# Retention with the wide product for q and k, split value products, and conversions queued behind normed rows at the hand-overs between stages

## The chip, the cores and the metric

The kernel runs on one core of a Trainium2 chip, in one launch. Its time is device microseconds (us) of that core. Before the change it takes 1206.07 us, the median of 3 runs (1205.51 to 1206.59). A core has five engines that run side by side, each through its own instructions in order: TensorE (PE, matrix products and transposes), VectorE (DVE), ScalarE (ACT), GpSimd (POOL) and SyncE (SP, which issues the transfers from memory). PEld is the part of TensorE that loads weights.

## The reference

Two transformer blocks over 256 tokens of width 1024, in fp32. The first mixes tokens with four kinds of attention and has an MLP; the second has a retention layer with a feed-forward part, and then a sparse-attention layer with another. Around each mixer and each feed-forward part stand a root-mean-square norm and a residual. What the change touches in the arithmetic is the retention layer:

```
proj = x @ w_in
q, k, v, g = split(proj)             # 4 heads; q, k 256 wide, v, g 512 wide
q = rotate_pairs(q, cos, sin)
k = rotate_pairs(k, cos, sin) * 256 ** -0.5
# chunks of 128 tokens:
scores = einsum('bhid,bhjd->bhij', qc, kc) * intra_decay
o = einsum('bhij,bhje->bhie', scores, vc) + (product with the state of the chunk before)
o = o * rsqrt(mean(o * o) + eps)     # per head
return (o * silu(g)) @ w_out
```

## The kernel before

**Split products.** fp32 matrix products are made of a high and a low part of each operand, both in the type fp32r. `each_half` (L225) fetches a piece of a weight (SP, tile `raw`, four buffers), ACT writes its high part (`whi`, L234) and DVE the low part (`wlo`, L237); there are six buffers of such pairs in the pool `wsp`, and some calls bring a private pool besides. `mm3` (L246) makes one product from three: L249, L250, L251. `ws_chunk` uses it with the weight as the stationary operand and 256 tokens as columns (N=256). `ws_wide` (L259) does the same with two matmuls: the high weight against the high and low tokens side by side (N=512, L268) and the low weight against the high tokens (N=256, L270); then ACT copies one half of the sum (L271) and DVE adds the other (L272).

**Norms and columns.** `a(t)` of a normed input takes the sum of squares of 128 tokens' rows (ACT L399, L401, DVE L404, L407, POOL L409), and DVE L193 and ACT L194 write the normed rows `xn`. `b(t)` transposes them on PE (L429), and for each of 8 columns ACT (L209) and DVE (L210) write high and low part with the norm's gain. In front of w_kv the rows serve two norms, and `b` writes two sets of columns.

**Hand-over between stages.** `project_back` (L350) multiplies back to width 1024. Its last weight halves are held: first they are run for tokens 0, then `residual(0)` (L442, or L451 and L454 with a norm) and `a(0)`; then for tokens 1, with `b(0)` ahead of the last half; then `residual(1)` and `a(1)`. The next stage is `an_groups` (L290): eight weight halves, j = 0 to 7, each with two pieces of `wlo`. It runs the first of them for tokens 0 and calls `b(1)` ahead of the last for which there is room, then tokens 1. This hand-over occurs five times: w_out to w_up, w_down to w_rv, w_ro to w_fi, w_fo to w_kv, w_no to w_fi.

**Order.** A scheduler puts each engine's instructions into one order when the program is built; on the chip each engine runs them in that order. `issue_after` fixes that an instruction stands behind another.

**Retention.** For each of four heads q and then k come from `ws_chunk` (w_rqk) and are rotated (DVE L1111, L1113, POOL L1114). The scores of a head (PE L1120, L1122, DVE L1123, an fp32 product) stand behind the next head's q. Then, for each head, the gates (w_rg, ACT L1138) and the value products (PE L1148, L1150, fp32, N=512), each of which is two instructions on PE.

Of the kernel before, what the change touches and what calls it, by code (L numbers as in the profile page):

```python
# [12 lines left out]
F32 = mybir.dt.float32  # L13
F32R = mybir.dt.float32r
BF = mybir.dt.bfloat16
AF = mybir.ActivationFunctionType
OP = mybir.AluOpType
AX = mybir.AxisListType

T = 256  # L20
# [192 lines left out]
class Kernel:  # L213
# [76 lines left out]
    def an_groups(self, groups, n, inp, order=(0, 1), extra=0):  # L290

        with ExitStack() as es:
            pool = self.pool(es, "ax_" + groups[0][0], extra) if extra else None
            hs = []
            for i, (name, g) in enumerate(groups):
                for j in range(4):
                    if j % 2 == 0:
                        own = {s: pool for s in range(2) if len(hs) + s + extra >= 4 * len(groups)}  # L300
                        chunk = self.each_half(name, 2 * g + j // 2, 4 * n, own, 2)
                    hs.append((i, 2 * j, next(chunk)))
            out = [[self.bank()[:, :n] for _ in range(2)] for _ in groups]

            def mul(j, t):
                i, k0, (hi, lo) = hs[j]
                for k in (k0, k0 + 1):
                    c = slice((k % 2) * n, (k % 2 + 1) * n)
                    self.as_mm(out[i][t], inp.x[0], k, (hi[:, c], lo[:, c]), k == 0, k == KT - 1, t)

            room = min(WSP + extra, len(hs))
            for j in range(room):
                if j == room - 1:
                    inp.b(1)
                mul(j, order[0])
            for j in range(len(hs)):
                if j >= room:
                    mul(j, order[0])
                mul(j, order[1])
        return out  # L320
# [29 lines left out]
    def project_back(self, name, nk, get, last, residual, nxt):  # L350


        accs = [[self.bank() for _ in range(2)] for _ in range(2)]
        n = nk // 2
        held = []
        with ExitStack() as es:
            wx = self.pool(es, "wx_" + name, 2 * last)
            for c in range(n):
                x, k0 = get(c)
                for s, half in enumerate(self.halves(name, c, pools={i: wx for i in range(2) if c >= n - last})):  # L360
                    a = (x, k0 + s, half, c == 0 and s == 0, c == n - 1 and s == 1)
                    if c < n - last:
                        for t in range(2):
                            self.as_t(accs[t], *a, t)
                    else:
                        held.append(a)
            for t in range(2):
                for banks in ((0,), (1,)) if t == 0 or not nxt else ((0, 1),):
                    for a in held[:-1]:
                        self.as_t(accs[t], *a, t, banks)  # L370
                    if t and nxt:
                        nxt.b(0)
                    self.as_t(accs[t], *held[-1], t, banks)
                residual(t, accs[t])
                if nxt:
                    nxt.a(t)


    def gain(self, name):
# [76 lines left out]
    def warm_up(self):  # L456
# [4 lines left out]
        for _ in range(WARM):  # L461
            self.nc.tensor.matmul(ps, w[:, :128], w, start=True, stop=True)

    def behind(self, engine):

        last = next(i for i in reversed(self.nc.cur_bb.bb.instructions) if i.engine == engine.engine)
        return self.tc.issue_after(last)


    def run(self):  # L470
        nc = self.nc
        with ExitStack() as es:
            self.cp = self.pool(es, "cp")
            self.wraw = self.pool(es, "wraw", RAW)
            self.wsp = self.pool(es, "wsp", WSP)
            self.rp = self.pool(es, "rp", 1)
            self.gp = self.pool(es, "gp", 3)
            self.xp = self.pool(es, "xp", 1)
            self.st = self.pool(es, "st", 3)
            self.scr = self.pool(es, "scr", 2)  # L480
            self.jp = self.pool(es, "jp", 1)
            self.ps = self.pool(es, "ps", 8, bass.MemoryType.PSUM)
            nc.scalar.preload_act_table_set("natural_log_exp_and_others")
            self.x = self.rp.tile([128, 2, D], F32, name="res")
            nc.sync.dma_start(self.x[:, 0, :], self.I["x"][:, 0, :])
            self.gc = self.cp.tile([128, len(PRE) * KT], F32, name="gc")
            nc.sync.dma_start(self.gc, self.I["gain_cols"])
            inp = Inputs(self, ("mix_norm_g",))
            cm = self.cp.tile([128, 512], F32, name="cm")
            nc.sync.dma_start(cm[:, :128], self.I["c_mat"][:, :128])  # L490
            self.ident, self.uge, self.ule, self.ones = [cm[:, i * 128:(i + 1) * 128] for i in range(4)]
            self.mhalf = self.cp.tile([128, 8], F32, name="mhalf")
            nc.gpsimd.memset(self.mhalf, -0.5)
            self.warm_up()
            inp.a(0)
            nc.sync.dma_start(self.x[:, 1, :], self.I["x"][:, 1, :])
            inp.b(0)
            inp.a(1)
            mx = self.mix(inp, cm)
            with ExitStack() as e1:  # L500
                inp = Inputs(self, ("mlp_norm_g",), (self.pool(e1, "xq0"),))
                self.project_back("w_out", KT, lambda c: (mx, 2 * c), 3, self.add_residual, inp)
                inp = self.mlp(inp)
            inp = self.retention(inp)
            with ExitStack() as e1:
                xq = self.pool(e1, "xq")
                inp = self.ffn(inp, 0, Inputs(self, ("kv", "pre1"), (None, xq)))
                inp = self.nsa(inp, xq)
            self.ffn(inp, 1, None)
# [564 lines left out]
    def retention(self, inp):  # L1074
        nc, I = self.nc, self.I
        mm = nc.tensor.matmul
        with ExitStack() as es:
# [27 lines left out]
                    pass  # L1105
            at = cp.tile([128, 4, 384], F32, name="at")

            def rotated(s, ps):
                a = tp.tile([128, 2, T], F32, tag=f"rot{s}", name="rot")
                b = tp.tile([128, 2, T], F32, tag="rotb", name="rotb")  # L1110
                nc.vector.tensor_tensor(a, ps, cs, op=OP.mult)  # L1111
                for j in range(2):
                    nc.vector.tensor_tensor(b[:, j, :], ps[:, 1 - j, :], sn[:, j, :], op=OP.mult)  # L1113
                nc.gpsimd.tensor_tensor(a, a, b, op=OP.add)  # L1114
                return a

# [9 lines left out]
            for h in range(4):  # L1126
                rot = []
                for s in range(2):
                    rot.append(rotated(s, self.ws_chunk("w_rqk", 2 * h + s, xin)))
                    if s == 0 and qk:  # L1130
                        scores(h - 1, *qk)
                qk = rot
            ys = []

            def gates(g):
                sg = tp.tile([128, 2, 512], F32, tag="sg", name="sg", bufs=1)
                for _ in self.an_steps("w_rg", g, 512, xin,
                                       lambda t, ps: nc.scalar.activation(sg[:, t, :], ps, AF.Silu)):  # L1138
                    pass
                return sg  # L1140

            def outputs(g, sg):
                vs = slice(g * 512, (g + 1) * 512)
                ss = self.st.tile([128, 2], F32, tag="ss2", name="ss2")
                po = []
                for t in range(2):
                    p = self.bank()
                    mm(p, at[:, g, t * 128:t * 128 + 128], v[:, 0, vs], start=True, stop=t == 0)  # L1148
                    if t:
                        mm(p, at[:, g, T:384], v[:, 1, vs], start=False, stop=True)  # L1150
                    junk = self.jp.tile([128, 2, 512], BF, tag="junk", name="junk")
                    nc.scalar.activation(junk[:, 0, :], p, AF.Square, accum_out=ss[:, t:t + 1])
                    po.append(p)
                r = self.rstd(ss, 512)
                yn = []
                for t in range(2):
                    u = up.tile([128, 512], F32, tag="yn", name="yn")
                    nc.vector.scalar_tensor_tensor(u, po[t], r[:, t:t + 1], sg[:, t, :], op0=OP.mult, op1=OP.mult)
                    yn.append(u)
                return yn  # L1160
# [7 lines left out]
            yn = None  # L1168
            for g in range(4):
                sg = gates(g)  # L1170
                if g == 0:
                    scores(3, *qk)
                else:
                    transposed(yn)
                yn = outputs(g, sg)

            e1.close()

# [408 lines left out]
```

## Time and profile before

| | |
|---|---|
| median of 3 runs | 1206.07 us (1205.51 to 1206.59) |
| profiled execution | 1207.36 us, its span 1205.5 us |
| granted TensorE clock, mean | 0.996 |
| PE busy | 1185.9 us, 98% |
| DVE busy | 799.0 us, 66% |
| ACT busy | 652.8 us, 54% |
| POOL busy | 80.1 us, 7% |

The profile is one execution; the span is from its first instruction to its last. Busy time is the time in which an engine runs at least one instruction. Matmuls overlap: an N=512 product is listed with some 390 ns, while the next starts sooner. So PE's pace is read from starts. "Idle before" names the time an engine waited ahead of an instruction and what released it. The granted clock is 1.00 at 2.4 GHz and 0.50 at 1.2 GHz.

### The profile page before, as it was taken

The page shows a single profiled execution, that of the slowest core. Times are in us where ns is not written, and L with a number is a line of the kernel's source. Part 1 is how long each engine was busy: PE and PEld are TensorE (multiplying, and loading weights), DVE is VectorE, ACT ScalarE, POOL GpSimd, SP SyncE. Part 2 cuts the span into 40 slices and gives each one's busy share as a digit, 9 for nine tenths or more (in the row PEclk, how much of TensorE's full clock was granted, in tenths as well). Part 3 has the DMA queues.
Part 4 walks back from the last instruction along what each step waited for, and adds up shares of the span by engine and source line. Part 5 has one row for each costly group of instructions (what it writes and reads, how often), then busy time and mean ns, then how long its engine had stood idle before and what let it go on. Part 6 is the DMA issues. An engine that isn't in the chain of part 4 may idle for free.

```text
span 1205.5 us, 18575 instructions
## 1 busy us (share of the span) xinstructions
PE 1185.9 (98%) x7104; PEld 1026.5 (85%) x7104; DVE 799.0 (66%) x1381; ACT 652.8 (54%) x1116; POOL 80.1 (7%) x87
## 2 busy tenths in 40 slices
PE   8999999999999999999999999999999999999997
PEld 6999999996888888899778888888889877888886
DVE  7757876557756668657556665657778967656663
ACT  6545764535544455543555554456567876645561
POOL 1000002100000000012000000000100530000000
PEclk8999999999999999999999999999999999999999
DMA  7654464446556666554546355556655226555560
GB/s 250 198 176 145 141 206 145 158 140 213 176 177 188 188 202 200 192 190 157 172 143 220 113 194 189 191 186 208 208 188 187 71 69 211 177 190 190 185 203 35
DMA packets 60777, 210.14 MB, mean 174 GB/s; under 512 B 7120, under 2 KB 9808, under 8 KB 60560
## 3 DMA queue, kind: packets, MB, share of 16 engines
q1 hardware_dynamic: 60688, 208.95, 53.5%
q8 instruction: 56, 0.92, 0.3%
q14 instruction: 33, 0.27, 0.1%
HBM read 207.84 MB, written 1.08 MB: 173 GB/s over the span
## 4 chain that ended last, share of the span: by engine, by line
PE 79%; DVE 8%; DMA 5%; ACT 5%; issue 2%; POOL 1%; SPq 0%; DVEq 0%; POOLq 0%; ACTq 0%
PE b L249 17%; PE b L251 17%; PE b L250 17%; PE b L268 13%; PE b L270 7%; DVE wlo L237 3%; ACT whi L234 2%; PE b L429 1%; DMA raw<-w_up 1%; PE b L1520 1%; DMA wng<-w_ng 1%; ACT s L1487 1%; PE b L1503 1%; PE b L1148 1%; DMA raw<-w_kv 1%
## 5 line engine op out<-in xcount | busy, mean ns | idle before, releaser
L237 DVE TENSOR_TENSOR wlo<-raw,whi 128x1024 fp32r<-128x1024 f32 (+3 forms) x432 | 474.3, 1111 | 267.2 <-ACT whi L234 264.2
L234 ACT ACTIVATE whi<-raw 128x1024 fp32r<-128x1024 f32 (+1 forms) x384 | 401.5, 1050 | 399.1 <-issue 118.7
L249 PE MATMUL b<-whi,x 128*128 128x512 f32 (+1 forms) x752 | 296.0, 395 | 4.0 <-ACT whi L234 2.5
L250 PE MATMUL b<-wlo,x 128*128 128x512 f32 (+1 forms) x752 | 292.8, 390 | 0.2
L251 PE MATMUL b<-whi,x 128*128 128x512 f32 (+1 forms) x752 | 291.9, 389 | 0.1
L268 PE MATMUL b<-x,whi 128*128 128x512 f32 x768 | 270.8, 396 | 0.0
L270 PE MATMUL b<-x,wlo 128*128 128x256 f32 x768 | 215.2, 280 | 0.0
L249 PE MATMUL b<-x,whi 128*128 128x256 f32 x736 | 210.9, 287 | 1.0 <-ACT x L242 1.0
L251 PE MATMUL b<-x,wlo 128*128 128x256 f32 x736 | 207.9, 283 | 0.4 <-DVE wlo L237 0.4
L250 PE MATMUL b<-x,whi 128*128 128x256 f32 x736 | 207.7, 282 | 0.0
L249 PEld LDWEIGHTS b<-whi,x 128*128 128x128 f32 x752 | 141.8, 189 | 38.0 <-ACT x L209 4.7
L268 PEld LDWEIGHTS b<-x,whi 128*128 128x128 f32 x768 | 144.2, 188 | 34.5
L251 PEld LDWEIGHTS b<-whi,x 128*128 128x128 f32 x752 | 141.7, 188 | 30.9 <-DVE x L243 1.2
L250 PEld LDWEIGHTS b<-wlo,x 128*128 128x128 f32 x752 | 142.0, 189 | 30.2 <-DVE wlo L237 2.4
L270 PEld LDWEIGHTS b<-x,wlo 128*128 128x128 f32 x768 | 144.7, 188 | 0.9
L249 PEld LDWEIGHTS b<-x,whi 128*128 128x128 f32 x736 | 140.4, 191 | 3.9 <-issue 2.0
L251 PEld LDWEIGHTS b<-x,wlo 128*128 128x128 f32 x736 | 140.5, 191 | 0.6 <-DVE wlo L237 0.6
L250 PEld LDWEIGHTS b<-x,whi 128*128 128x128 f32 x736 | 140.5, 191 | 0.2
L409 POOL TENSOR_TENSOR rstd<-ms,mhalf 128x1 f32<-128x1 f32 x22 | 14.1, 640 | 690.2 <-DVE ms L407 690.2
L210 DVE SCALAR_TENSOR_TENSOR x<-b,gc,x 128x128 fp32r<-128x128 f32 x112 | 36.8, 348 | 19.2 <-ACT x L209 17.2
L209 ACT ACTIVATE x<-b,gc 128x128 fp32r<-128x128 f32 x112 | 38.2, 368 | 19.5 <-PE b L429 14.7
L1487 ACT ACTIVATE s<-s,nm 128x128 f32<-128x128 f32 (+1 forms) x64 | 28.3, 446 | 2.6 <-DVE rz L1491 1.4
(269 smaller groups left out, 930.3 us busy)
## 6 DMA issues: line engine op xcount, KB each, us to landing
raw<-w_fi SPq DMA_DIRECT2D x88, 512.0 KB, 4.5
raw<-w_fo SPq DMA_DIRECT2D x44, 512.0 KB, 4.5
raw<-w_gate SPq DMA_DIRECT2D x32, 512.0 KB, 3.7
raw<-w_up SPq DMA_DIRECT2D x32, 512.0 KB, 4.7
raw<-w_down SPq DMA_DIRECT2D x32, 512.0 KB, 4.6
raw<-w_qk SPq DMA_DIRECT2D x24, 512.0 KB, 4.0
raw<-w_rv SPq DMA_DIRECT2D x16, 512.0 KB, 5.0
raw<-w_rqk SPq DMA_DIRECT2D x16, 512.0 KB, 4.5
```

What stands on the lines that cost most here:

```text
L209: k.nc.scalar.activation(hi, ps[:, j, :], AF.Copy, scale=g)
L210: k.nc.vector.scalar_tensor_tensor(lo, ps[:, j, :], g, hi.bitcast(F32), op0=OP.mult, op1=OP.subtract)
L234: nc.scalar.activation(hi[:, :n], r, AF.Copy)
L237: nc.vector.tensor_tensor(lo[:, c], r[:, c], hi[:, c].bitcast(F32), op=OP.subtract)
L249: mm(out, lhs[0], rhs[0], start=start, stop=False)
L250: mm(out, lhs[0], rhs[1], start=False, stop=False)
L251: mm(out, lhs[1], rhs[0], start=False, stop=stop)
L268: mm(ps.rearrange("p a t -> p (a t)"), half[0][:, s], x[2][:, k].rearrange("p a t -> p (a t)"), start=k == 0, stop=False)
L270: mm(ps[:, 0], half[1][:, s], x[0][:, k, :], start=False, stop=k == KT - 1)
L409: nc.gpsimd.tensor_tensor(r, ms, self.mhalf[:, :1], op=OP.pow)
L429: self.nc.tensor.transpose(ps[:, j, :], src[:, j * 128:(j + 1) * 128], self.ident)
L1487: nc.scalar.activation(s[:, a, i, :], s[:, a, i, :], AF.Exp, bias=nm[:, a, i:i + 1], scale=-1.0, accum_out=z[:, a, i:i + 1])
```

## The change

Three things. First, the retention's q and k come from `ws_wide`; since its result lies in SBUF and not in a PSUM bank, the rotation reads it there. Second, the value products are made with `mm3`: in `gates`, behind the first weight half, both value tiles and the scores are split in high and low parts, in the buffers of the rotation; the last head's scores stand there too, behind that first half. Third, `project_back` notes the last ACT and DVE instruction of `a(0)` ("a") and of `b(0)` ("b"). In the next `an_groups` the conversions j = 2 to 4 are put behind "a", those from 5 on behind "b"; `residual(1)` and `a(1)` are put behind "b" as well. Ahead of the first `an_groups` no step is noted, and it stays as it is.

```diff
@@ an_groups
                 for j in range(4):
+                    queued = self.conversions_behind(len(hs))
...
-                    hs.append((i, 2 * j, next(chunk)))
+                    with queued:
+                        hs.append((i, 2 * j, next(chunk)))
@@ project_back
                     if t and nxt:
                         nxt.b(0)
+                        self.steps["b"] = self.lasts()
                     self.as_t(accs[t], *held[-1], t, banks)
-                residual(t, accs[t])
-                if nxt:
-                    nxt.a(t)
+                with self.queued(self.steps["b"] if t and nxt else ()):
+                    residual(t, accs[t])
+                    if nxt:
+                        nxt.a(t)
+                if nxt and not t:
+                    self.steps["a"] = self.lasts()
@@ new helpers
+    def lasts(self):
+        order = list(reversed(self.nc.cur_bb.bb.instructions))
+        return [next(i for i in order if i.engine == e.engine) for e in (self.nc.scalar, self.nc.vector)]
+    def queued(self, instructions):
+        es = ExitStack()
+        for i in instructions:
+            es.enter_context(self.tc.issue_after(i))
+        return es
+    def conversions_behind(self, j):
+        return self.queued(self.steps.get("a" if j < 5 else "b", ()) if j > 1 else ())
@@ retention
-            def rotated(s, ps):
-                a = tp.tile([128, 2, T], F32, tag=f"rot{s}", name="rot")
+            def rotated(s, i):
+                a = self.ws_wide("w_rqk", i, xin, tp.tile([128, 2, T], F32, tag=f"rot{s}", name="rot"))
                 b = tp.tile([128, 2, T], F32, tag="rotb", name="rotb")
-                nc.vector.tensor_tensor(a, ps, cs, op=OP.mult)
                 for j in range(2):
-                    nc.vector.tensor_tensor(b[:, j, :], ps[:, 1 - j, :], sn[:, j, :], op=OP.mult)
+                    nc.vector.tensor_tensor(b[:, j, :], a[:, 1 - j, :], sn[:, j, :], op=OP.mult)
+                nc.vector.tensor_tensor(a, a, cs, op=OP.mult)
...
-                    rot.append(rotated(s, self.ws_chunk("w_rqk", 2 * h + s, xin)))
+                    rot.append(rotated(s, 2 * h + s))
...
             def gates(g):
                 sg = tp.tile([128, 2, 512], F32, tag="sg", name="sg", bufs=1)
+                parts = None
                 for _ in self.an_steps("w_rg", g, 512, xin,
                                        lambda t, ps: nc.scalar.activation(sg[:, t, :], ps, AF.Silu)):
-                    pass
-                return sg
+                    if parts is None:
+                        if g == 0:
+                            scores(3, *qk)
+                        src = [v[:, t, g * 512:(g + 1) * 512] for t in range(2)] + [at[:, g, :]]
+                        parts = []
+                        for tag, x in zip(("rot0", "rot1", "rotb"), src):
+                            hl = [...]
+                            self.split(*hl, x)
+                            parts.append(hl)
+                return sg, parts
...
-                    mm(p, at[:, g, t * 128:t * 128 + 128], v[:, 0, vs], start=True, stop=t == 0)
+                    self.mm3(p, [x[:, t * 128:t * 128 + 128] for x in w], v0, True, t == 0)
                     if t:
-                        mm(p, at[:, g, T:384], v[:, 1, vs], start=False, stop=True)
+                        self.mm3(p, [x[:, T:384] for x in w], v1, False, True)
```

In the kernel after the change the lines L399 to L454 stand 6 further on (L442 is L448, L401 is L407, L404 is L410), and L1054 is L1078; L193, L194, L209, L210, L234 and L237 stay.

DVE at the hand-over from w_down to w_rv, before, from the first normed row (L193) on; x_4937 are the columns of the new input, res the residual:

```order
L193 TENSOR_SCALAR xn<-res,rstd 128x512
L210 SCALAR_TENSOR_TENSOR x_4937<-b,gc,x_4937 128x128 x3
L442 TENSOR_TENSOR res<-res,b 128x512
L210 SCALAR_TENSOR_TENSOR x_4937<-b,gc,x_4937 128x128 x2
L442 TENSOR_TENSOR res<-res,b 128x512
L210 SCALAR_TENSOR_TENSOR x_4937<-b,gc,x_4937 128x128 x2
L404 ISA junk,ss<-res 128x512
L404 ISA ss 128x1
L210 SCALAR_TENSOR_TENSOR x_4937<-b,gc,x_4937 128x128
L407 TENSOR_SCALAR ms<-ss 128x1
L237 TENSOR_TENSOR wlo<-raw,whi 128x512
```

The same place on DVE after the change:

```order
L193 TENSOR_SCALAR xn<-res,rstd 128x512
L237 TENSOR_TENSOR wlo<-raw,whi 128x512 x4
L210 SCALAR_TENSOR_TENSOR x_4937<-b,gc,x_4937 128x128 x2
L237 TENSOR_TENSOR wlo<-raw,whi 128x512
L210 SCALAR_TENSOR_TENSOR x_4937<-b,gc,x_4937 128x128 x2
L237 TENSOR_TENSOR wlo<-raw,whi 128x512
L210 SCALAR_TENSOR_TENSOR x_4937<-b,gc,x_4937 128x128 x4
L448 TENSOR_TENSOR res<-res,b 128x512 x2
L237 TENSOR_TENSOR wlo<-raw,whi 128x512
L410 ISA junk,ss<-res 128x512
```

Six pieces of conversion have moved in among the eight columns, and the residual's two adds, which stood between columns, stand behind the last of them.

ACT at the hand-over from w_fo to w_kv, before, from the normed row (L194) of tokens 0 to that of tokens 1; x_8359 and x_8360 are the two sets of columns:

```order
L194 ACTIVATE xn<-res,rstd 128x512
L209 ACTIVATE x_8359<-b,gc 128x128 x3
L399 ACTIVATE junk,ss<-b 128x512
L209 ACTIVATE x_8359<-b,gc 128x128 x2
L401 ACTIVATE junk,ss<-b 128x512
L209 ACTIVATE x_8359<-b,gc 128x128 x2
L209 ACTIVATE x_8360<-b,gc 128x128
L209 ACTIVATE x_8359<-b,gc 128x128
L399 ACTIVATE junk,ss<-res 128x512
L209 ACTIVATE x_8360<-b,gc 128x128 x6
L194 ACTIVATE xn<-res,rstd 128x512
```

The same place on ACT after the change, with the two sets named x_8343 and x_8344:

```order
L194 ACTIVATE xn<-res,rstd 128x512
L234 ACTIVATE whi<-raw 128x1024 x3
L209 ACTIVATE x_8343<-b,gc 128x128 x8
L209 ACTIVATE x_8344<-b,gc 128x128 x8
L405 ACTIVATE junk,ss<-b 128x512
L407 ACTIVATE junk,ss<-b 128x512
L234 ACTIVATE whi<-raw 128x1024
L405 ACTIVATE junk,ss<-res 128x512
L242 ACTIVATE wg<-wng 128x8x48
L194 ACTIVATE xn<-res,rstd 128x512
```

Three conversions now stand ahead of the columns, and the sums of squares of tokens 1 behind all sixteen of them.

## Rows read from the trace of the kernel before

**Rows 1.** The page's chain that ended last: share of the span by engine

```profile
PE 79%; DVE 8%; DMA 5%; ACT 5%; issue 2%; POOL 1%; SPq 0%; DVEq 0%; POOLq 0%; ACTq 0%
```

**Rows 2.** Windows: stretch, then its length, busy us (instructions) by engine, clock, DMA

```profile
515.00:590.00 75.00, 75.00 (x517) 69.49 (x516) 45.33 (x53) 30.29 (x33) 14.67 (x8) 1.00 0.55 176
586.00:645.00 59.00, 59.00 (x258) 45.17 (x257) 32.43 (x38) 31.38 (x50) 2.80 (x4) 1.00 0.45 143
```

**Rows 3.** Timeline of PE, q and k: start, duration, engine, line, operation

```profile
528.93 0.28 PE L251 MATMUL b<-x,wlo 128*128 128x256 f32 x1
...
540.46 0.28 PE L251 MATMUL b<-x,wlo 128*128 128x256 f32 x1
```

**Rows 4.** Timeline of PE, wide products of w_fi

```profile
702.31 0.28 PE L270 MATMUL b<-x,wlo 128*128 128x256 f32 x1
...
707.62 0.28 PE L270 MATMUL b<-x,wlo 128*128 128x256 f32 x1
```

**Rows 5.** Groups by line, 700 to 840: count, busy, mean ns, idle before

```profile
L271 ACT ACTIVATE sg<-b 128x256 f32<-128x256 f32 x18 | 6.6, 367 | 0.5 <-PE b L270 0.5
...
L272 DVE TENSOR_TENSOR sg<-b,sg 128x256 f32<-128x256 f32 x17 | 7.1, 418 | 0.0
```

**Rows 6.** Timeline of PE, value products of head 0

```profile
586.94 1.88 PE L1148 MATMUL b<-v,at 128*128 128x512 f32 x4
588.66 1.02 PE L1150 MATMUL b<-v,at 128*128 128x512 f32 x2
```

**Rows 7.** Timeline of DVE, ACT and PE, w_down to w_rv

```profile
468.05 2.55 DVE L237 TENSOR_TENSOR wlo<-raw,whi 128x512 fp32r<-128x512 f32 x4 [1.58 <-ACT whi L234]
470.51 1.28 DVE L442 TENSOR_TENSOR res<-res,b 128x512 f32<-128x512 f32 x2
...
476.65 0.48 DVE L193 TENSOR_SCALAR xn<-res,rstd 128x512 f32<-128x512 f32 x1 [0.66 <-POOL rstd L409]
...
480.52 0.68 DVE L442 TENSOR_TENSOR res<-res,b 128x512 f32<-128x512 f32 x1
...
487.45 0.49 DVE L193 TENSOR_SCALAR xn<-res,rstd 128x512 f32<-128x512 f32 x1 [0.73 <-POOL rstd L409]
...
477.95 1.94 ACT L209 ACTIVATE x<-b,gc 128x128 fp32r<-128x128 f32 x5 [0.57 <-PE b L429]
...
477.29 1.06 PE L429 MATMUL b<-cm,xn 128*128 128x128 f32 x8 [0.59 <-DVE xn L193]
...
488.00 1.09 PE L429 MATMUL b<-cm,xn 128*128 128x128 f32 x8
```

**Rows 8.** Timeline of ACT and PE, w_fo to w_kv

```profile
864.42 1.15 ACT L209 ACTIVATE x<-b,gc 128x128 fp32r<-128x128 f32 x3 [1.75 <-PE b L429]
...
866.70 0.61 ACT L401 ACTIVATE junk<-b 128x512 bf16<-128x512 f32 x1
...
873.47 0.72 ACT L194 ACTIVATE xn<-res,rstd 128x512 f32<-128x512 f32 x1 [0.38 <-POOL rstd L409]
...
874.37 1.09 PE L429 MATMUL b<-cm,xn 128*128 128x128 f32 x8
...
878.44 0.50 PE L249 MATMUL b<-whi,x 128*128 128x512 f32 x1 [0.83 <-ACT x L209]
```

**Rows 9.** Timeline of ACT and PE, w_out to w_up

```profile
290.86 1.06 ACT L234 ACTIVATE whi<-raw 128x1024 fp32r<-128x1024 f32 x1 [3.77 <-DMA raw<-w_up]
...
291.32 0.39 PE L251 MATMUL b<-whi,x 128*128 128x512 f32 x1
...
298.79 0.40 PE L251 MATMUL b<-whi,x 128*128 128x512 f32 x1
```

**Rows 10.** Windows of PE at the start: length, busy (instructions), clock, DMA

```profile
5.50:9.00 3.50, 0.03 (x1) 0.82 0.95 348
9.00:14.50 5.50, 5.50 (x18) 0.50 0.84 291
```

More of the change, by code (lines that the diff above doesn't have):

```diff
@@ L482, in run @@
             self.ps = self.pool(es, "ps", 8, bass.MemoryType.PSUM)
+            self.steps = {}
             nc.scalar.preload_act_table_set("natural_log_exp_and_others")
@@ L1136, in gates, with outputs @@
                 sg = tp.tile([128, 2, 512], F32, tag="sg", name="sg", bufs=1)
+                parts = None
                 for _ in self.an_steps("w_rg", g, 512, xin,
                                        lambda t, ps: nc.scalar.activation(sg[:, t, :], ps, AF.Silu)):
-                    pass
-                return sg
-            def outputs(g, sg):
-                vs = slice(g * 512, (g + 1) * 512)
+                    if parts is None:
[4 more added lines that the diff above has]
+                        for tag, x in zip(("rot0", "rot1", "rotb"), src):
+                            hl = [tp.tile([128, 2, T], F32, tag=tag, name=tag).rearrange("p a t -> p (a t)").bitcast(F32R)
+                                  [:, :x.shape[1]] for _ in range(2)]
+                            self.split(*hl, x)
+                            parts.append(hl)
+                return sg, parts
+            def outputs(g, sg, parts):
+                v0, v1, w = parts
                 ss = self.st.tile([128, 2], F32, tag="ss2", name="ss2")
@@ L1170, in retention @@
                 sg = gates(g)
-                if g == 0:
-                    scores(3, *qk)
-                else:
+                if g:
                     transposed(yn)
-                yn = outputs(g, sg)
+                yn = outputs(g, *sg)
             e1.close()
```

## The prediction, made before the changed kernel ran

> **What bounds the kernel now.** I read the page first. Its chain of waits runs through TensorE (PE) for 79% of the span [rows 1], and no other engine has more than a tenth of it. So a change here is worth what it takes off PE's instructions, plus what it does to the few moments at which PE stands still. The busy times by stretch come second: in the retention's q and k stage and in its output stage PE has no gap at all, while VectorE (DVE) is busy 45.33 of 75 us and 32.43 of 59 us, and ScalarE (ACT) less [rows 2]. Work added to those two engines is hidden there, and only PE's instructions count. Third come the timelines of PE, DVE and ACT around the places where `project_back` hands over to `an_groups`. There PE does wait: 0.59 us for DVE's first half of the normed rows before w_rv [rows 7], 0.83 us for a column before w_kv [rows 8]. The reader should see that these are small, and that the engines run their instructions in the written order: what is put ahead of a normed row or a column delays it.
>
> **q and k.** The old form runs three N=256 products for each of 16 halves x 8 steps = 128 steps. From 528.93 to 540.46 stand 96 of them, 32 trios, so a trio is 11.53 / 32 = 0.360 us [rows 3]. The wide pair runs elsewhere in this kernel: 15 pairs from 702.31 to 707.62, 0.354 each [rows 4]. 128 x 0.006 = -0.8 us. The wide form adds an ACT copy (0.37) and a DVE add (0.42) for each of 16 halves [rows 5], 5.9 and 6.7 us, on engines with 45 and 30 us free in that stretch. The rotation now waits for the add before it starts, about 1 us later per head, but the scores that need it stand a whole chunk of q, 16 pairs or 5.7 us, behind it. For the last head they now stand behind the first half of the gates. Bounds: -1.0 (the pair a little quicker) to +1.6 (the scores wait 0.4 for each of four heads, one DVE add). I take -0.8, since the idle time is large.
>
> **Value products.** Each head has three fp32 products with N=512, two PE instructions each: four take 586.94 to 588.66, 0.43 each, so six take 2.58 and four heads 10.3 us [rows 6]. After it there are nine fp32r products per head, 36 in all. An N=512 one is the wide pair less an N=256 one, 0.354 - 0.120 = 0.234 [rows 3, 4], so 8.4 us: -1.9 us. The splits are three conversions per head on each of ACT and DVE, at some 0.65 us for 512 columns (four such pieces take 2.55 [rows 7]): 2 us per head beside 13 us of gates. Bounds: -2.5 to 0 (PE then waits as long for a split as it saves).
>
> **The queueing.** Five hand-overs are touched. What is removed is work ahead of the first normed rows; what is added stands ahead of the columns, and behind these now stand residual(1) and a(1), whose rows b(1) transposes. PE runs `b(1)` before the last half that fits, so PE waits for whatever comes late there.
>
> *w_out to w_up.* ACT's half of the normed rows stood behind a conversion that had idled 3.77 us for its DMA [rows 9]. From 291.32 to 298.79 PE starts 21 N=512 products and 8 transposes: 21 x 0.23 + 1.1 = 5.9 of 7.47 us, so 1.6 us are waits [rows 7, 9]. The conversion now stands behind; I take -1.6 (bounds -1.6 and 0).
>
> *w_down to w_rv.* Four pieces of conversion held DVE from 468.05 until the residual could start at 470.51 [rows 7]. They go behind the row, so the row comes up to 1.15 us sooner, and PE's 0.59 us wait goes. But then ACT runs three conversions, 3 x 1.05, before the first column. Its half of the row now ends at about 476.2, the conversions at 479.4, eight columns at 0.39 each (five took 1.94 [rows 7]) at 482.5; DVE's eight, with its own pieces between them, end near 483.4. Before, the residual's second add was already running at 480.52, between the columns; now both wait for the last column, and the second starts at about 484.0, 3.5 us later. From that add to the row it was 6.93 us [rows 7]. The three columns that stood in it (0.9) are gone, two more conversion pieces (1.2) are in it: row at 491.2 or later, the transposes half a us behind, 491.9 where they had begun at 488.00. PE has nothing else in its order: +3.9 us, which swallows the early gain. Bounds: -0.6 (only the wait goes) to +5.
>
> *w_kv.* Here b writes two sets of columns, 16 on each engine. ACT was free from 862.67, 1.75 before the column at 864.42 [rows 8]. Three conversions end at 865.8, 16 columns at 0.39 at 872.1, and only then come the sums of squares that before ran between columns; L401 (now L407) starts near 872.9 instead of 866.70. From there to the row it was 6.77 us with ten DVE columns of about 0.3 in between [rows 8]; without these, and with three conversion pieces of 0.6, 5.6 us: row at about 878.5 to 879.0, transposes at 879.4 against 874.37. That is +5.0, of which 0.9 us only replaces the wait at 878.44 [rows 8]: +4.1. Bounds: -0.9 to +5.5.
>
> *The two w_fi hand-overs.* They have the same order with two halves of private space, so PE reaches b(1) later. Nearest rows: 0 where the slack covers all, +3.9 as at w_rv. I take +1.0 each, +2.0.
>
> **Sum.** -0.8 - 1.9 - 1.6 + 3.9 + 4.1 + 2.0 = +5.7 us. The profiled execution took 1207.36 us, 1.29 above the median of 1206.07, its span 1205.5; the difference is carried over to the median: 1211.8.
>
> **Rivals.**
>
> *Only the waits go.* If the conversions fit into gaps of DVE and ACT behind the rows, and b(1) still comes in time, the hand-overs give -1.6, -0.6, -0.9 and nothing at w_fi, with -2.7 from retention: -5.8, 1200.3. For it: ACT and DVE are both far from full, and the rows do come sooner. Against it: before, these conversions already ran while the engines had nothing else (DVE's four pieces end with the add behind them); the change takes that time away and puts the work where columns and rows compete.
>
> *Break-even.* The columns come late by half of what I work out: +4.2 at the hand-overs, -4.3 from w_out and the retention, 1206. That needs shorter queues than those listed; for it speaks only that each of my starts is worked out by hand.
>
> *The clock falls (slower still).* My sum leaves PE idle for some 4 us at w_rv and 5 at w_kv. At the start of this run PE is idle from 5.5 to 9.0, and in the next 5.5 us its granted clock is 0.50, the 1.2 GHz level [rows 10]; so half of that time, 2.7 us, is lost after such an idle stretch. It decides where an idle stretch reaches that 3.5 us: one fall gives 1214.5, two 1217.2. The Trainium skill, "TensorE: Matmul & The Clock Gate", section "What's actually happening", says that TensorE runs at 1.2 GHz by default and activity releases it, an idle stretch bringing it back; the start of this run agrees (0.50), and no later wait here is long enough to show it. Against: if part of b(1)'s delay is covered, no idle stretch is that long.
>
> *Retention stalls (not what the split is for).* If DVE's adds and POOL's rotation make PE wait for the scores, the -2.7 becomes up to +1.6: the forecast would be 1216. Against it: the free time in [rows 2].
>
> **How the numbers follow.** Late b(1) with the clock held, 1209 to 1214: 0.42. Late b(1) with one or two falls, 1214 to 1217.5: 0.24, with it retention stalls: 0.03. Break-even, 1203.7 to 1208.5: 0.14. Only the waits go, 1200 to 1203.7: 0.17. 0.2%, 2.4 us, is about what a measurement of this kernel tells from no change; of break-even 0.11 lies within it and 0.03 on the fast side. So slower 0.69, same 0.11, faster 0.20. The range leaves out half of the fast case and the top: 1202 to 1216.5; the likeliest case alone is 1209 to 1214.
>
> **What would show it.** In the profile after: transposes of b(1) at w_rv and w_kv that wait for the row (L193 or L194), with PE idle 3 to 5 us each; no idle in front of b(0)'s transposes; three L234 between L194 and the first L209; the residual's adds (L448, L460) behind all columns; the q and k stretch with pairs of 0.354; nine N=512 products per head at 0.23 in place of six at 0.43. The forecast is wrong if b(1)'s transposes start without a wait, or if the retention stretch is not some 2.7 us shorter.

## The result, and the profile after

The changed kernel takes 1223.57 us, the median of 4 runs (1221.63 to 1223.91), against 1206.33 for the kernel before: 1.0136 of its time, with a 95% interval of 1.0123 to 1.0149, so 17.2 us slower. The direction was forecast, the size was not: 5.7 us had been worked out, and the range ended at 1216.5. The profiled execution took 1221.63 us, its span 1219.9.

First the hand-over from w_down to w_rv, in the timeline of ACT, DVE, SyncE's queue (SPq) and PE of the changed kernel (start, duration, engine, line; in brackets the idle time before it and what ended it):

```profile
475.51 2.94 ACT L234 ACTIVATE whi<-raw 128x1024 fp32r<-128x1024 f32 x3
478.35 0.60 ACT L209 ACTIVATE x<-b,gc 128x128 fp32r<-128x128 f32 x2
...
485.91 1.06 ACT L234 ACTIVATE whi<-raw 128x1024 fp32r<-128x1024 f32 x1 [2.72 <-DMA raw<-w_rv]
486.88 0.61 ACT L405 ACTIVATE junk<-res 128x512 bf16<-128x512 f32 x1
...
474.88 0.49 DVE L193 TENSOR_SCALAR xn<-res,rstd 128x512 f32<-128x512 f32 x1 [0.66 <-POOL rstd L415]
476.58 2.50 DVE L237 TENSOR_TENSOR wlo<-raw,whi 128x512 fp32r<-128x512 f32 x4 [1.22 <-ACT whi L234]
...
482.55 1.28 DVE L448 TENSOR_TENSOR res<-res,b 128x512 f32<-128x512 f32 x2
...
487.62 0.21 DVE L413 TENSOR_SCALAR ms<-ss 128x1 f32<-128x1 f32 x1 [1.98 <-ACT junk L405]
...
492.55 0.49 DVE L193 TENSOR_SCALAR xn<-res,rstd 128x512 f32<-128x512 f32 x1 [0.73 <-POOL rstd L415]
...
479.18 0.33 SPq L231 DMA_DIRECT2D raw<-w_rv  x1
...
476.01 1.04 PE L435 MATMUL b<-cm,xn 128*128 128x128 f32 x8
...
493.09 1.97 PE L435 MATMUL b<-cm,xn 128*128 128x128 f32 x8 [5.07 <-DVE xn L193]
```

The first transposes no longer wait, where there were 0.59 us [rows 7]. Three conversions stand ahead of the columns, and the residual's adds behind them, as worked out. What was not worked out is the line at 485.91: a fourth conversion stands on ACT ahead of the sum of squares (L405) of tokens 1 and idles 2.72 us for its transfer. That transfer was issued at 479.18, just behind the four late pieces of conversion on DVE (476.58 to 479.08), the last of which freed its buffer, and it landed 6.7 us later. DVE waits 1.98 us for the sum, and PE stands idle 5.07 us.

The hand-over from w_fo to w_kv, in the same view:

```profile
888.72 0.52 ACT L242 ACTIVATE wg<-wng 128x384 fp32r<-128x384 f32 x1 [4.30 <-DMA wng<-w_ng]
889.15 0.71 ACT L194 ACTIVATE xn<-res,rstd 128x512 f32<-128x512 f32 x1
...
886.87 0.49 DVE L193 TENSOR_SCALAR xn<-res,rstd 128x512 f32<-128x512 f32 x1 [0.66 <-POOL rstd L415]
...
881.60 0.44 SPq L1305 DMA_DIRECT2D wng<-w_ng  x1
...
882.48 0.50 PE L249 MATMUL b<-whi,x 128*128 128x512 f32 x1 [0.65 <-ACT whi L234]
884.93 0.50 PE L250 MATMUL b<-wlo,x 128*128 128x512 f32 x1 [1.95 <-DVE wlo L237]
...
887.41 1.11 PE L435 MATMUL b<-cm,xn 128*128 128x128 f32 x4
889.91 1.12 PE L435 MATMUL b<-cm,xn 128*128 128x128 f32 x4 [1.39 <-ACT xn L194]
```

Here PE waits for three late things in turn: the two parts of a queued conversion, then half of the row, which stands on ACT behind the split of a small weight, `wng`, that idles 4.30 us for its transfer. Before, b(1) began at 874.37, and a column behind that split cost PE 0.83 us [rows 8].

The windows of PE behind the two (length, busy, instructions, granted clock, DMA):

```profile
487.00:493.00 6.00, 1.02 (x5) 0.78 0.55 198
493.00:499.00 6.00, 5.91 (x22) 0.66 0.13 50
...
881.00:890.00 9.00, 4.64 (x15) 0.79 0.95 295
890.00:896.00 6.00, 6.00 (x22) 0.74 0.02 8
```

After each long wait the granted clock falls: 0.66 and 0.74 of full speed over 6 us, so some part of each stretch at the 1.2 GHz level. 6 x 0.34 + 6 x 0.26 = 3.6 us of PE's time are lost there by these windows. At the start of the run the clock also fell behind an idle stretch [rows 10].

In the retention stage, the scores' products on PE and the rotation's add on POOL that they wait for, and the value products of head 0:

```profile
572.01 2.31 POOL L1138 TENSOR_TENSOR rot<-rot,rotb 128x512 f32<-128x512 f32 x1 [5.00 <-DVE rot L1137]
...
585.45 2.33 POOL L1138 TENSOR_TENSOR rot<-rot,rotb 128x512 f32<-128x512 f32 x1 [6.14 <-DVE rot L1137]
...
574.38 1.13 PE L1144 MATMUL b<-rot 128*128 128x256 f32 x4 [0.61 <-POOL rot L1138]
...
587.83 1.13 PE L1144 MATMUL b<-rot 128*128 128x256 f32 x4 [1.77 <-POOL rot L1138]
...
595.63 0.39 PE L249 MATMUL b<-rot,rotb 128*128 128x512 f32 x1
...
597.68 0.39 PE L249 MATMUL b<-whi,x 128*128 128x512 f32 x1
```

Nine value products take 597.68 - 595.63 = 2.05 us, where six took 2.58 [rows 6]: 0.53 x 4 = 2.1 us gained. But the scores of the last two heads wait for POOL. From start to start these waits cost 0.77 and 1.93 us, 2.7 us in all.

### The profile page after: what moved, and what is told of

Read it like the earlier page. It is cut to its first block, busy times and chain, and to the rows that moved or that the text cites. A ratio compares the mean times of both kernels' runs of the same rounds, so it can differ in the third digit from the quotient of the medians.

```text
span 1219.9 us, 18420 instructions
## 1 busy us (share of the span) xinstructions
PE 1191.4 (98%) x6988; PEld 1024.3 (84%) x6988; DVE 814.4 (67%) x1409; ACT 661.0 (54%) x1144; POOL 78.3 (6%) x87
## 4 chain that ended last, share of the span: by engine, by line
PE 82%; DVE 8%; ACT 3%; DMA 3%; issue 2%; POOL 1%; SPq 1%; DVEq 0%; POOLq 0%; ACTq 0%
PE b L249 17%; PE b L268 17%; PE b L250 17%; PE b L251 17%; PE b L270 8%; DVE wlo L237 3%; PE b L435 1%; ACT whi L234 1%; DMA raw<-w_no 1%; PE b L1553 1%; POOL rstd L415 1%; ACT s L1520 1%; PE b L1536 1%; DMA wng<-w_ng 1%; DMA raw<-w_rv 1%
## 5 line engine op out<-in xcount | busy, mean ns | idle before, releaser
L237 DVE TENSOR_TENSOR wlo<-raw,whi 128x1024 fp32r<-128x1024 f32 (+3 forms) x432 | 475.2, 1113 | 256.9 <-ACT whi L234 253.1
L234 ACT ACTIVATE whi<-raw 128x1024 fp32r<-128x1024 f32 (+1 forms) x384 | 400.1, 1050 | 380.2 <-issue 114.0
L268 PE MATMUL b<-x,whi 128*128 128x512 f32 x896 | 316.3, 397 | 0.0
L268 PEld LDWEIGHTS b<-x,whi 128*128 128x128 f32 x896 | 168.3, 188 | 40.3
L249 PE MATMUL b<-x,whi 128*128 128x256 f32 x608 | 174.4, 287 | 1.0 <-ACT x L242 1.0
L250 PE MATMUL b<-x,whi 128*128 128x256 f32 x608 | 171.5, 282 | 0.0
L249 PEld LDWEIGHTS b<-x,whi 128*128 128x128 f32 x608 | 115.9, 191 | 3.9 <-issue 2.0
L250 PEld LDWEIGHTS b<-x,whi 128*128 128x128 f32 x608 | 116.0, 191 | 0.1
L209 ACT ACTIVATE x<-b,gc 128x128 fp32r<-128x128 f32 x112 | 36.8, 364 | 19.8 <-PE b L435 10.8
L210 DVE SCALAR_TENSOR_TENSOR x<-b,gc,x 128x128 fp32r<-128x128 f32 x112 | 35.7, 347 | 10.6 <-ACT x L209 9.2
```

The lines of the kernel that those rows point to most:

```text
L209: k.nc.scalar.activation(hi, ps[:, j, :], AF.Copy, scale=g)
L210: k.nc.vector.scalar_tensor_tensor(lo, ps[:, j, :], g, hi.bitcast(F32), op0=OP.mult, op1=OP.subtract)
L234: nc.scalar.activation(hi[:, :n], r, AF.Copy)
L237: nc.vector.tensor_tensor(lo[:, c], r[:, c], hi[:, c].bitcast(F32), op=OP.subtract)
L249: mm(out, lhs[0], rhs[0], start=start, stop=False)
L250: mm(out, lhs[0], rhs[1], start=False, stop=False)
```

## The experiments

Each run stood beside the kernel before on the same chip; ratios are to it, with 95% intervals. "Theory A" is that the queueing makes all of the loss.

**The parts.** `e1_ret` has only the retention's part of the diff, `e2_queue` only the queueing. In `e3_conv` the residual's queue is empty, in `e4_resid` that of the conversions:

```diff
# e3_conv, from e2_queue
-                with self.queued(self.steps["b"] if t and nxt else ()):
+                with self.queued(()):
# e4_resid, from e2_queue
-        return self.queued(self.steps.get("a" if j < 5 else "b", ()) if j > 1 else ())
+        return self.queued(())
```

> The kernel before with the retention part of the change alone (wide q and k, split value products), no queueing. Theory A (the queueing costs everything, retention is even): the gates gain 1.9 us, q and k 0.8, and the waits of the scores for the last two heads (0.77 and 1.93 us in the changed kernel's trace) give 2.7 back: 1206.3, no change. Rival B (the waits of the scores come only from the disturbed start of the stage that the queueing leaves): the 2.7 us stay as a gain, 1203.6. Rival C (retention is itself a good part of the loss): 1209 or more.

Measured: 1206.37 us, 1.0001 (0.9992 to 1.0011). Its trace has the same two waits of the scores, 0.77 and 1.92 us. So retention is even, and the waits are its own: rival B falls, and rival C with it.

> The kernel before with all of the queueing and the old retention. Theory A: all of the loss of 17.2 us is here, about 1222 to 1224. Rival C (retention carries 3 us or more of it): 1220 or less. In the trace of both: b(1) at w_rv and w_kv waits some 5 us, and the granted clock falls behind it.

Measured: 1221.98 us, 1.0126 (1.0107 to 1.0145). The loss is here. The waits are shorter than expected: in its trace PE idles 3.53 us for L193 at w_rv, and 0.66, 1.95 and 0.49 us in turn at w_kv.

> The kernel before with the conversions queued, but residual(1) and a(1) not queued. Theory A (both queues add up in one chain: columns late by the conversions, residual late by the columns): with the residual free to run between columns the rows of tokens 1 come 3 us sooner at w_rv and w_kv, 1211 to 1216. Rival D (the conversions alone make the loss, by what they delay on ACT and by the transfers that they hold up): 1220 or more. Rival E (the conversions cost nothing by themselves): 1205, since only the early gains at the first rows stay.

Measured: 1214.06 us, 1.0071 (1.0055 to 1.0088), within what theory A gave. At w_rv its row of tokens 1 is in time. At w_kv, in this execution, the conversions' queue is enough for the loss, as rival D has it. PE waits 2.62 us for a column behind the split of `wng`, whose transfer comes late:

```profile
881.99 0.52 ACT L242 ACTIVATE wg<-wng 128x384 fp32r<-128x384 f32 x1 [3.94 <-DMA wng<-w_ng]
...
864.28 1.03 PE L435 MATMUL b<-cm,xn 128*128 128x128 f32 x8
...
882.83 0.50 PE L249 MATMUL b<-whi,x 128*128 128x512 f32 x1 [2.62 <-ACT x L209]
...
1016.27 1.03 PE L435 MATMUL b<-cm,xn 128*128 128x128 f32 x8
```

From b(0) at w_kv to b(0) at the next hand-over it takes 1016.27 - 864.28 = 151.99 us. The changed kernel takes 152.05 (871.64 to 1023.69), the kernel before 146.38 (863.78 to 1010.16).

> The kernel before with residual(1) and a(1) queued behind b(0), and the conversions left where they were. Theory A: the residual is late by the columns left to run, 1 to 3 us at each of w_rv and w_kv, less at the others: 1208 to 1212. Rival D (the conversions alone make the loss): 1206, no change.

Measured: 1210.30 us, 1.0038 (1.0023 to 1.0052): the residual's queue costs by itself, which rival D denied. In its trace PE waits 1.66 us at w_rv and 2.64 us at w_kv for L193. But from b(0) at w_kv to b(0) at the next hand-over it takes 146.60 us (864.90 to 1011.50), as good as before the change: the wait there does not show in the stage's length. The two alone make 0.0109, both together 0.0126; in the profiles of both alone the clock stays at 1.00 at these places, in `e2_queue` it falls to 0.54 behind w_rv.

**The scores' waits.** `e5_add` and `e6_late` start from `e1_ret`:

```diff
# e5_add
-                nc.gpsimd.tensor_tensor(a, a, b, op=OP.add)
+                nc.vector.tensor_tensor(a, a, b, op=OP.add)
# e6_late
-                    if parts is None:
+                    step += 1
+                    if step == (2 if g == 0 else 1):
```

> The retention part alone (as e1_ret), with the rotation's last add on DVE in place of POOL. Theory P (the scores wait for POOL's add, 2.31 us long where DVE works beside it): the two waits of 0.77 and 1.92 us of e1_ret go or shrink to 0.4 together, 2.3 us less than e1_ret, about 1204.0. Rival Q (the scores are late because the k of the last head is late on ACT and DVE, behind conversions and splits): the second wait keeps 1 us or more, about 1205 to 1206.

Measured: 1203.93 us, 0.9972 (0.9960 to 0.9985). The timeline of PE for these scores:

```profile
566.25 1.02 PE L1120 MATMUL b<-rot 128*128 128x256 f32 x4
...
578.06 1.10 PE L1120 MATMUL b<-rot 128*128 128x256 f32 x4
```

Neither waits. Theory P holds: with POOL's add out of the path retention gains 3.4 us (1.8 to 4.8), and the 2.7 forecast for it lie within that.

> The retention part alone (as e1_ret), with the last head's scores and the first head's splits behind the second half of the gates and not the first. If the wait of 1.92 us is only a matter of how much stands between k and its scores, it goes (4.5 us more are between) and the 0.77 us of the third head stays: 1.9 us less than e1_ret, about 1204.4. If the splits then come late for the value products, PE waits there and the time is that of e1_ret, 1206.3.

Measured: 1206.69 us, 0.9996 (0.9985 to 1.0008). The expectation fell. In the timeline of PE and POOL the wait is shorter, but the add still starts late and takes 2.35 us:

```profile
583.02 1.13 PE L1120 MATMUL b<-rot 128*128 128x256 f32 x4 [0.87 <-POOL rot L1114]
...
580.62 2.35 POOL L1114 TENSOR_TENSOR rot<-rot,rotb 128x512 f32<-128x512 f32 x1 [6.13 <-DVE rot L1113]
```

The scores of the second head waited too, 0.78 us from start to start. Behind k's last pair stand 24 of the gates' products here, where `e1_ret` has 20: some 0.9 us more, not the 4.5 that the edit was meant to put in. So what a longer distance would give stays open.

**The clock and the transfer at w_rv**, both from the changed kernel:

```diff
# e7_fill, in transposed(), for b(1) at w_rv alone
+        if fill is not None:
+            for _ in range(20):
+                self.nc.tensor.matmul(ps.rearrange("p k t -> p (k t)"), fill[:, :128], fill[:, :512], start=True, stop=True)
# e8_free
-                    queued = self.conversions_behind(len(hs))
+                    queued = self.queued(self.steps["c"]) if name == "w_rv" and len(hs) > 5 else self.conversions_behind(len(hs))
-                if nxt and not t:
-                    self.steps["a"] = self.lasts()
+                if nxt:
+                    self.steps["c" if t else "a"] = self.lasts()
```

> The changed kernel with 20 products N=512 of no use, 4.5 us, ahead of b(1)'s transposes at w_rv, into the bank that the transposes then write; PE works in the time in which it stood idle. Theory K (the idle stretch drops the clock, and that costs 2 us behind it): the clock behind b(1) stays at 1.00 in place of 0.66, 2.0 us less, about 1221.5. Rival L (the clock after an idle stretch costs nothing measurable, since PE waits anyway for columns): no change, 1223.5.

Measured: 1221.15 us, 1.0117 (1.0099 to 1.0134). The interval overlaps that of the changed kernel, so the trace decides:

```profile
487.00:493.00 6.00, 5.43 (x25) 1.00 0.54 181
493.00:499.00 6.00, 5.98 (x30) 1.00 0.12 45
```

The clock stays at 1.00 with PE at useless work in the same idle time. The transposes of b(1) start at 492.90, 0.19 earlier than in the changed kernel, and those of the first gated output, 114 us on, at 606.55 instead of 608.57: 2.0 us sooner. 1.8 us are the clock's. Theory K holds.

> The changed kernel with one difference: at w_rv the conversions from j = 6 on stand behind a(1), not only behind b(0). Theory M (at w_rv the sum of squares of tokens 1 stood behind a conversion that idled 2.72 us for its transfer, which could only start when the late conversions gave their buffers back): b(1) at w_rv comes 2.5 us sooner; with the clock perhaps held another 2 us, 1219 to 1221. Rival N (the row of tokens 1 is bound by columns and residual alone): b(1) comes 1 us sooner or less, 1222.5 or more.

Measured: 1219.16 us, 1.0095 (1.0078 to 1.0112). In its timeline of ACT and PE the conversion that waited stands no longer ahead of the sum of squares:

```profile
482.64 1.05 ACT L234 ACTIVATE whi<-raw 128x1024 fp32r<-128x1024 f32 x1
483.82 0.63 ACT L405 ACTIVATE junk<-res 128x512 bf16<-128x512 f32 x1
...
490.67 1.09 PE L435 MATMUL b<-cm,xn 128*128 128x128 f32 x8 [2.15 <-DVE xn L193]
```

b(1) starts at 490.67 instead of 493.09, 2.4 us sooner, though this execution was 0.5 us behind at b(0) (476.51 against 476.01). So 2.9 us are gained between the two. The idle time is not gone, and the clock still falls (0.75 in 493 to 499). Theory M holds. By the first gated output 2.5 us of the gain are left (606.60 against 608.57); the medians differ by 4.4, and what makes the rest is not shown.

**w_kv, and what w_up was worth.** `e9_best` is `e5_add` with the conversions queued at w_up only, `e10_wng` has a transfer moved besides, `e11_nokv` is the changed kernel without the queueing at w_kv, and `e12_wng` is the changed kernel with the edit of `e10_wng`:

```diff
# e9_best, from e5_add and the conversions' queue
+                    queued = self.conversions_behind(len(hs)) if name.startswith("w_up") else self.queued(())
# e10_wng, from e9_best: these two lines stand ahead of tz now, and no longer ahead of the split
+            raw = tp.tile([128, KT * 48], F32, name="wng")
+            nc.sync.dma_start(raw, I["w_ng"])
# e11_nokv
+                    queued = self.conversions_behind(len(hs)) if name != "w_kv" else self.queued(())
+                with self.queued(self.steps["b"] if t and nxt and name != "w_fo0" else ()):
```

> The retention part with the rotation's add on DVE (as e5_add), and the conversions queued at the hand-over to w_up alone; the residual is not queued anywhere. If what the traces show adds up (-2.4 to -3.1 from retention, -1.7 at w_up), 4 to 4.8 us less than the kernel before. Rival: the conversions moved at w_up delay a later row there, and it gives 1 us or nothing; then 2.4 to 3.1 less.

Measured: 1204.16 us, 0.9981 (0.9970 to 0.9992), no better than `e5_add` without any queueing (0.9972). The rival's size held: at w_up the queue gives nothing that the times can tell. Its reason, a later row, is not shown. The timeline of `e1_ret`, where that hand-over is as before, shows another, that the wait is gone without the queue as well:

```profile
289.07 1.06 ACT L234 ACTIVATE whi<-raw 128x1024 fp32r<-128x1024 f32 x1 [2.36 <-DMA raw<-w_up]
290.03 0.71 ACT L194 ACTIVATE xn<-res,rstd 128x512 f32<-128x512 f32 x1
...
292.26 1.03 PE L429 MATMUL b<-cm,xn 128*128 128x128 f32 x8
```

Its transposes run in one piece: the half row is there in time, since the conversion ahead of it idles 2.36 us and not 3.77. From the first transposes of the run to those of b(1) at w_up the execution profiled before takes 296.34 us (8.97 to 305.31). Three others without the conversions' queue there (`e1_ret`, `e4_resid`, `e5_add`) take 295.03 to 295.17, and the nine with it 294.29 to 294.88. So most of the wait belonged to that one execution, and some 0.5 us are left for the queue.

> As e9_best, with the small weight w_ng of the w_kv stage fetched ahead of the four constants that stand before it in its queue. Before, ACT's split of it idled 1.13 us for its transfer between the columns of b(1), and PE lost 0.99 us there. If that transfer is the cause, 1 us less than e9_best; if the columns are late anyway, no change.

Measured: 1201.77 us, 0.9953 (0.9937 to 0.9970), the shortest of all. PE's wait of 1.14 us behind the split in `e9_best` is gone. The medians differ by 2.4 us, the profiled executions by 0.86 (1202.73 and 1201.87); the intervals touch, so about 1 us is shown by the traces, and the rest stays open.

> The changed kernel without any queueing at the hand-over from w_fo to w_kv, the rest as it is. By the trace of the changed kernel that hand-over takes 6.5 to 7.3 us more than before (transposes of b(1) 5.2 later, then the row's second half behind w_ng's transfer and the lower clock): 6.5 to 7 us less than the changed kernel, about 1217. Rival, the size forecast for it: 4.1 us, about 1219.5.

Measured: 1216.89 us, 1.0079 (1.0061 to 1.0097), 6.7 us less than the changed kernel. So that hand-over costs 6.7 by the medians, where 4.1 was forecast; the two intervals together leave about 4 to 9.5. From b(0) there to the next hand-over it takes 144.63 us (872.07 to 1016.70), 7.4 less than the changed kernel.

> The changed kernel with w_ng fetched ahead of the four constants that stand before it in SP's queue (the edit of e10_wng). In the changed kernel the second half of the row of tokens 1 stood on ACT behind w_ng's split, which idled 4.30 us for that transfer, and PE lost 1.70 us there. If that transfer is the excess over my price of this hand-over, 1.5 to 3 us less than the changed kernel, 1220.5 to 1222. Rival: the transfer still has to wait behind two weight pieces that get their buffers only from the late conversions, the split now stands ahead of columns, and the wait only moves: no change, 1223.5, or slower.

Measured: 1222.47 us, 1.0124 (1.0107 to 1.0141), no change that can be told. The rival held: on ACT the split now idles 2.21 us ahead of six columns, and b(1) starts at 888.06, 18.1 us behind b(0) (869.99). In the changed kernel its second half stood 18.3 us behind b(0) (871.64 to 889.91). Behind late conversions an earlier place in the queue only moved the wait.

## Why the prediction was wrong

**The mechanism was right in the main.** Late columns, a late residual, PE idle at b(1): at w_rv the forecast's case is what happened, and with it the rival of the falling clock. At w_kv the late row came too, but PE stood still ahead of it for other things. What failed are sizes of terms of the sum, nearly all in one direction, and one path that it did not have: the transfers that late conversions hold up.

**w_up, -1.6.** The row showed a wait that for the most part belonged to that one execution. `e1_ret` loses it untouched, and `e9_best` gains nothing that its time can tell. By the traces the term is about -0.5.

**w_rv, +3.9.** The row moved as worked out up to the residual (second add near 483.2; 484.0 was forecast, less the 0.5 us by which this execution was ahead, 475.77 against 476.30 for PE's last product ahead of b(0)). From there to the row I counted conversions by their durations, 7.2 us; it was 9.4. The step that failed is "From that add to the row it was 6.93 us": a fourth conversion in front of L405 waited for its transfer, and that could not have started before the late conversions gave their buffers back. `e8_free` puts 2.9 us on it. From PE's last product ahead of b(0) to b(1) the change costs 5.6 us here (475.77 to 493.09, before 476.30 to 488.00). The prediction had named DMA waits at w_up and not asked which transfers the queued conversions would hold up.

**The clock, a rival at 0.24.** It fell at both places. At w_rv it cost 1.8 us by `e7_fill`; at w_kv the window gives 1.6. The forecast worked out idle stretches of 4 and 5 us beside a row that showed a fall after 3.5 us [rows 10], and yet left the clock out of its sum: by its own rows it belonged in it. Of the Trainium skill, "TensorE: Matmul & The Clock Gate", section "What's actually happening", the traces bear out that idle time brings the low level back.

**w_kv, +4.1.** The first half of b(1)'s transposes began 5.2 us later than the hand-over before it had already moved them (871.64 against 863.78 for b(0), 887.41 against 874.37 for b(1)); 5.0 was forecast. The row itself came as worked out: 878.5 to 879.0 were forecast, to which come the 7.9 us by which b(0) was late already, and DVE's half started at 886.87. But the sign named for it, PE idle 3 to 5 us for the row, is not there: PE stood still for the parts of a queued conversion ahead of it (0.65 and 1.95 us), and then for the row's other half. What I took off, 0.9 for the wait behind `wng`, did not go: its transfer was issued at 881.60, before at 869.56, 12 us earlier. SyncE came to the stage's constants at 874.50 in place of 866.28, behind weight pieces that waited for buffers. It then took 5.61 us in place of 1.78 to issue the second of them, for which no row shows the reason. The split idled 4.30 us, and half of the row stood behind it. With the clock, 6.7 us in all (`e11_nokv`). The step that failed is the path: the term ran through the late residual alone, and `e3_conv`, which does not queue the residual, is as slow from b(0) at w_kv on. That b(1)'s shift came out at the 5.0 forecast is in part luck.

**w_fi, +2.0.** From the first transposes of b(0) to the next stage PE falls back 1.5 us at the first (676.32 and 683.08, then 701.64 and 709.91), 0.8 at the second. No run tried these alone.

**Retention, -2.7.** Both gains are there, 0.9 from pairs (31 pairs from 531.65 to 542.60 are 0.353 each) and 2.1 from values. The step that failed is "the scores that need it stand a whole chunk of q behind it", which counted DVE's add and not POOL's rotation beside a busier DVE. The rival that named POOL had 0.03. My upper bound of +1.6 for q and k was too low as well, with waits of 2.7 less a gain of 0.9. `e5_add` gives the 2.7 us back.

Put right, the sum is -0.5 (w_up) + 5.6 (w_rv) + 1.8 (clock at w_rv) + 6.7 (w_kv) + 2.3 (w_fi) + 0 (retention) = 15.9 us, against 17.2 measured (interval 14.8 to 18.0). The two profiled executions differ by only 14.3 (1221.63 and 1207.36); what makes the other 3 us of the medians no trace shows. One figure of the rivals does not come out either: half of 3.9, 4.1 and 2.0 is 5.0, not the +4.2 of the break-even case, whose time changes little by it.

## What to carry to other kernels

When work is queued later, follow what it gives back as well as what it takes: the buffer that it frees, the transfer that waits for that buffer, and whatever stands behind that transfer's reader in an in-order queue. An idle stretch that a sum works out should be held against the row that shows where the clock fell, in the sum itself and not only among the rivals. And a wait in one profiled execution is worth a term only if other executions show it too; here more than 1 of 1.6 us was that one execution's own.

## What the runs showed of the hardware that was not expected

POOL's add of 128x512 took 1.28 to 1.29 us (at 565.73 and 578.03 of the changed kernel) when it began first, and 2.31 to 2.33 when a DVE conversion had begun just before it: at 585.45 POOL, at 585.43 DVE, whose 1.23 us are about the difference. The loser can be DVE as well: at 559.34 POOL took 1.28 us and DVE's conversion 2.36.

```profile
585.45 2.33 POOL L1138 TENSOR_TENSOR rot<-rot,rotb 128x512 f32<-128x512 f32 x1 [6.14 <-DVE rot L1137]
585.43 1.23 DVE L237 TENSOR_TENSOR wlo<-raw,whi 128x1024 fp32r<-128x1024 f32 x1
...
559.34 1.28 POOL L1138 TENSOR_TENSOR rot<-rot,rotb 128x512 f32<-128x512 f32 x1 [5.03 <-DVE rot L1137]
559.34 2.36 DVE L237 TENSOR_TENSOR wlo<-raw,whi 128x1024 fp32r<-128x1024 f32 x1
```

The Trainium skill, "SBUF — State Buffer", section "SBUF: two separate sides", says that DVE operations with two SBUF inputs and POOL share one pair of ports, which the first holds for its whole instruction while the other is blocked; these numbers agree.

The clock also fell where a single idle stretch was short: in `e8_free` PE waited 2.15 us, ran eight transposes and waited a little more, and the next window still has 0.75. In `e4_resid` a wait of 2.64 us before transposes left it at 1.00.
